# Two-layer hybrid backbone: the recurrent units hold their inverse and their transposed factors in tiles that they already have, and buffer and bank reserves are set anew

## The chip, the cores and the metric

One core of one Trainium2 chip runs the whole program. The metric is the device time of one execution in microseconds (us). The program is one launch with all weights in HBM; the profile shows one execution by the five engines of the core (TensorE, VectorE = DVE, ScalarE = ACT, GpSimd = POOL, SyncE = SP, which issues nearly all DMAs).

## What is computed

Two layers work on two streams of 256 tokens (context `s = 0`, latents `s = 1`), width 2048, all in float32. Each layer: a modulated RMS norm, one input projection (2048 x 5888), three head groups on its columns, a gate on each, one output projection (2048 x 2048), post norm and residual. Layer 1 gives only the latents, so of the context it needs only keys, values and the final recurrent state.

```python
def hybrid_layer(x, xc, c, c_ctx, cos, sin, lp, need_ctx_out):
    ...
    p = split_columns(h @ lp['w_in'])
    pc = split_columns(hc @ lp['w_in'])
    ...
    Sf_c, of_c = rwkv_scan(S0, r_c, vv_c, kk_c, *dirs_c[0], reverse=False)
    Sb_c, ob_c = rwkv_scan(S0, r_c, vv_c, kk_c, *dirs_c[1], reverse=True)
    _, of_l = rwkv_scan(Sf_c, r_l, vv_l, kk_l, *dirs_l[0], reverse=False)
    _, ob_l = rwkv_scan(Sb_c, r_l, vv_l, kk_l, *dirs_l[1], reverse=True)
    ...
    y = jnp.concatenate([att_l, rw_l, pool_l], axis=-1) @ lp['w_out']
```

The group that the change touches is the recurrence (`rwkv_scan`, 8 heads of 64, both directions): per token `S = S*w - (S kk)(kk a)^T + v k^T`, output `S r`.

## The kernel before

**A planner orders everything.** Each kind of work is a Python generator (`Worker`) that yields operations and tile requests. `Scheduler.run` (L543) keeps a model of engine times, takes at each step the ready operation that starts first in 40 ns slots with a bonus by priority (`PRIO`, L209: weight split and post norm 6, scan 5, back, elim, fin and attention 4, front 3, projection 0), and emits it; so each engine's instruction order is fixed when the program is built. All instructions are issued in one helper, so the profile gives line L587 (L332 for memsets) to nearly all of them, and groups are told apart by tile names. `HELD` (L207) is the extra time the model gives to an operation whose partitions start elsewhere than those of the one before on the same engine.

**Buffers.** Tile classes share pools (L121 to L130). `h`, `y`, `sp`, `wf`, `rf`, `rb`, `at`, `aq`, `lo`, `ev` and others take 2 KB slots of one pool of 77 (`SB_BYTES` less the constants and the other pools, L121). The PSUM classes `acc`, `ada`, `pr`, `scan`, `att`, `st` share 8 banks. `PHASES` (L131) gives each class a reserve in each phase: up to it a request is granted if a slot is free; beyond it only if the reserves that others haven't used still fit (`Scheduler.alloc`, L421). The sums of the reserves exceed 77 in the phases `first` to `second`, so there a class hardly gets more than its reserve. A request that isn't granted stops its worker, and a tile is free again when its last user is emitted. Phases in order: `start`, `turned`, `first` (layer 0 projections), `rested`, `between` (projection of layer 0 done), `turn` (first output pass prepared), `second` (set by `post_work` when the latents of layer 1 are modulated), `third` (layer 1 needs its context input no more), `last`.

**Projections.** `main_work` takes weight tiles (split by ACT into a rounded high part and by DVE into the rest, `w_split`) and issues three matmuls per 128 x 128 block: `acc<-h,sp` is the input projection (512 columns in layer 0, 256 per stream in layer 1), `acc<-sp,h` the output projection (512 columns), 384 matmuls for each of three passes (l, s) = (0, 0), (0, 1), (1, 1). Three column groups of layer 1's context part are issued ahead of the second half of pass (0, 1). The last pass needs the recurrence's rows last in its first half (`MIX_ORDER`).

**A recurrent unit** is (layer, head pair g, stream s): 16 units, 8 per layer, in the order of `UNITS`. Tokens are cut in four chunks of 64. Units run through five workers, one unit at a time in each:

- `front` (L1291): decays, keys and rates; fills `BK` (2 `rf` tiles), `W` (4 `rf` tiles, 2 where the unit gives no output, `need` false: the context units of layer 1), last `RS` (1 `rf` tile), from `psv`, a `pr` bank that it holds until `RS` is written. It asks for no `rf` tile until `back` has taken up the unit before.
- `back` (L1407): the products of `BK` and `W`, two `pr` banks per direction, masked by DVE into `UB` (2 `rb` tiles, 1 without `need`) and `W`; copies the diagonal 32 x 32 blocks to `N0`; transposes `BK` on TensorE into `W2` (2 `rb` tiles), frees `BK`; takes `Z` (1 `rb` tile) and clears it on POOL (L1455).
- `elim` (L1458): inverts the unit triangular diagonal blocks on DVE, 31 steps of two dependent operations (`tp<-dt,tp`, `tp<-tp`) after two large transposes (`dt<-tp`).
- `fin` (L1487): eight ACT copies of the inverted diagonal blocks into `Z`, then the off-diagonal blocks by 64 matmuls of 32 x 32 (`psY` from `UB`, `psZ`) and four ACT copies into `Z`. Without `need` it frees `UB`.
- `scan` (L1530): per chunk `psX` from `W` and `RS`, `psS` from `Z`, `psN` from `W2`, `psO` from `W` and `UB`, copies and state updates in between; at its end frees `RS`, `W`, `UB`, `W2`, `Z`; then a group norm and `rg_work`, whose result is a row of the output projection's input.

So a unit with output holds 7 `rf` tiles from `front` on, 5 of them and 5 `rb` tiles from the end of `back` to the end of `scan`. Without output these numbers are 5, then 3 `rf` and 4 `rb` (3 after `fin`). The reserves of `rf`/`rb` are 12/5 in `first` and `second`, 14/5 in `between` and `last`, 9/5 in `turn`.

Of the kernel before, what the change touches and what calls it, by code (L numbers as in the profile page):

```python
# [25 lines left out]
T = SEQ + CTX  # L26
# [75 lines left out]
def layout(a):  # L102
# [38 lines left out]
}  # L141
# [64 lines left out]
BACK = 60.0  # L206
HELD = 120.0  # L207
HOLD = {None: 1000.0, "ada": 3000.0}
# [418 lines left out]
class Hybrid:  # L627
# [779 lines left out]
    def back(self, l, g, s, need, RS, W, BK, PC, bv):  # L1407
        V, S, G, T, D_ = self.V, self.S, self.G, self.T, self.D
        ident = self.k("ident")
        UB = []  # L1410
# [28 lines left out]
        for q in range(4):  # L1439
            b = q % 2  # L1440
            for d in range(2):
                yield S.copy(out=N0[Q[q], d], in_=UB[d][Q[q], :, 0, 32 * b:32 * b + 32])
        W2 = []
        for d in range(2):
            z = yield Alloc("rb", (128, 4, 2, 64))
            W2.append(z)
            psW = yield Alloc("pr", (128, 512))
            for c in range(4):
                yield T.transpose(out=psW[:, 128 * c:128 * c + 128], in_=BK[d][:, c].rearrange("p a b -> p (a b)"), identity=ident)
            yield S.copy(out=W2[d].rearrange("p c h k -> p (c h k)"), in_=psW)  # L1450
            self.free(psW)
        self.free(*BK)

        Z = yield Alloc("rb", (128, 2, 4, 64))
        yield G.memset(out=Z, value=0.0)  # L1455
        self.push(self.bq, (N0, (l, g, s, need, RS, W, UB, W2, Z, PC, bv)))

# [28 lines left out]

    def fin(self, T1, T2, l, g, s, need, RS, W, UB, W2, Z, PC, bv):  # L1487
        V, S, G, T = self.V, self.S, self.G, self.T
        for q in range(4):
            b = q % 2  # L1490
            yield S.copy(out=Z[Q[q], 0, :, 32 * b:32 * b + 32], in_=T1[Q[q], 0].rearrange("p c u -> p u c"))
            yield S.copy(out=Z[Q[q], 1, :, 32 * b:32 * b + 32], in_=T2[Q[q], 1])
        psY = yield Alloc("pr", (128, 512))
        for u in range(4):
            for p in range(2):
                q0, q1 = Q[2 * p], Q[2 * p + 1]
                o = slice(32 * u, 32 * u + 32)
                yield T.matmul(out=psY[q1, o], lhsT=UB[0][q0, u, 0, 32:64], rhs=T2[q0, 0, u, :], start=True, stop=True)
                yield T.matmul(out=psY[q0, o], lhsT=UB[1][q1, u, 0, 0:32], rhs=T1[q1, 1, :, u], start=True, stop=True)
        YS = yield Alloc("tp", (128, 4, 32))  # L1500
        yield S.copy(out=YS.rearrange("p u t -> p (u t)"), in_=psY[:, 0:128])
        self.free(psY)
        psZ = yield Alloc("pr", (128, 512))
        for u in range(4):
            for p in range(2):
                q0, q1 = Q[2 * p], Q[2 * p + 1]
                o = slice(32 * u, 32 * u + 32)
                yield T.matmul(out=psZ[q0, o], lhsT=YS[q1, u, :], rhs=T1[q1, 0, :, u], start=True, stop=True)
                yield T.matmul(out=psZ[q1, o], lhsT=YS[q0, u, :], rhs=T2[q0, 1, u, :], start=True, stop=True)
        psz3 = psZ[:, 0:128].rearrange("p (u t) -> p u t", u=4)  # L1510
        for p in range(2):
            yield S.copy(out=Z[Q[2 * p], 0, :, 32:64], in_=psz3[Q[2 * p]])
            yield S.copy(out=Z[Q[2 * p + 1], 1, :, 0:32], in_=psz3[Q[2 * p + 1]])
        self.free(psZ, YS, T1, T2)
        if not need:
            self.free(*UB)
            UB = []
        self.push(self.pq, (l, g, s, need, RS, W, UB, W2, Z, PC, bv))

# [9 lines left out]

    def scan(self, Sc, l, g, s, need, RS, W, UB, W2, Z, PC, bv):  # L1530
        V, S, G, T, D_ = self.V, self.S, self.G, self.T, self.D
# [11 lines left out]
        for i in range(4):  # L1543
# [15 lines left out]
            for d in range(2):  # L1559
                for p in range(2):  # L1560
                    yield T.matmul(out=psS[H[p], 64 * d:64 * d + 64], lhsT=Z[H[p], d, c[d], :], rhs=X[H[p], 64 * d:64 * d + 64], start=True, stop=True)
            self.free(X)
# [35 lines left out]
            if need:  # L1598
# [5 lines left out]
                self.free(psO)  # L1604
        self.free(RS, *W[0], *W[1], *UB, *W2, Z, PC)
        if need:
# [340 lines left out]
```

## Time and profile before

| what | value |
|---|---|
| median of 3 executions | 1768.84 us (1763.94 to 1772.35) |
| profiled execution, its own time | 1770.03 us |
| its span, first to last instruction | 1768.1 us |
| mean granted TensorE clock | 0.981 |
| TensorE matmul busy | 1675.5 us (95%) |
| VectorE busy | 1350.8 us (76%) |
| ScalarE busy | 926.8 us (52%) |
| GpSimd busy | 16.0 us (1%) |
| DMA | 350.03 MB, mean 198 GB/s |

The profile's rows give a group's or an instruction's engine, line, operation, output tile `<-` input tiles, shape and count, with its time; "idle before" is the idle time of that engine ahead of it and what ended it. A busy TensorE is not one at its peak, since matmuls are pipelined and their ends modelled. Stages of the span: start and first modulation to 142 us; layer 0's input projection to 911; output passes (0, 0) and (0, 1) with the first groups of layer 1 to 1146; layer 1's input projection to 1633; output pass (1, 1) to 1756; post norm and stores to the end.

### The profile page before, as it was taken

To read this page: it belongs to the slowest core of one execution; us is meant where nothing else is said; L and a number is where in the kernel's file an instruction comes from. 1 tells how busy PE (TensorE), PEld (TensorE's weight loads), DVE (VectorE), ACT (ScalarE), POOL (GpSimd) and SP (SyncE) were. 2 spreads that over 40 slices of the span, in tenths; PEclk is the share of its full clock that TensorE was granted. 3 is DMA by queue.
4 is the path that set the end of the run, shared out by engine and by line. 5 is a ranking of instruction groups with operands and counts; after the bars stand their busy time and mean duration, and the time that the engine had idled before them with its cause. 6 is when DMAs were issued, how large, how long until landed. Compare 5 with 4: busy or idle time off the path is not lost.

```text
span 1768.1 us, 38232 instructions
## 1 busy us (share of the span) xinstructions
PE 1675.5 (95%) x13658; PEld 1330.3 (75%) x13658; DVE 1350.8 (76%) x4249; ACT 926.8 (52%) x2278; POOL 16.0 (1%) x93
## 2 busy tenths in 40 slices
PE   4999999999999999999999999999999999999977
PEld 3677677666766676667777888899999888888765
DVE  3335888867897869697767685899689999999863
ACT  5324455434554445345446574575455676666541
POOL 0000000000000000000000000000000000000000
PEclk9999999999999999999999999999999999999988
DMA  9993674657364945574669965665434536555642
GB/s 343 362 365 105 206 227 155 225 185 247 120 221 148 277 149 171 170 238 148 207 223 351 328 191 169 199 202 177 147 102 157 155 98 204 153 165 185 215 132 95
DMA packets 218094, 350.03 MB, mean 198 GB/s; under 512 B 22896, under 2 KB 62128, under 8 KB 217904
## 3 DMA queue, kind: packets, MB, share of 16 engines
q1 hardware_dynamic: 217904, 347.60, 60.2%
q8 instruction: 107, 1.75, 0.4%
q14 instruction: 83, 0.68, 0.1%
HBM read 316.54 MB, written 30.97 MB: 197 GB/s over the span
## 4 chain that ended last, share of the span: by engine, by line
PE 72%; DVE 12%; DMA 10%; ACT 2%; issue 2%; SPq 1%; DVEq 0%; POOL 0%; ACTq 0%
PE acc L587 50%; PE scan L587 6%; PE pr L587 5%; PE att L587 5%; PE ada L587 4%; DVE tp L587 3%; DMA wa<-in_ada_w_dram 2%; DVE sp L587 2%; DMA w<-in_ada_w_dram 2%; DVE q L587 1%; DVE rf L587 1%; DMA wf<-in_w_out_dram 1%; DMA wf<-in_w_in_dram 1%; PE st L587 1%; DMA sp<-w 1%
## 5 line engine op out<-in xcount | busy, mean ns | idle before, releaser
L587 PE MATMUL acc<-h,sp 128*128 128x256 f32 (+1 forms) x5088 | 971.1, 339 | 14.1 <-DMA sp<-w 5.6
L587 PEld LDWEIGHTS acc<-h,sp 128*128 128x128 f32 x5088 | 755.4, 190 | 133.9 <-issue 24.3
L587 DVE TENSOR_TENSOR sp<-wf,sp 128x512 fp32r<-128x512 f32 (+1 forms) x568 | 362.4, 664 | 96.4 <-ACT sp L587 90.2
L587 ACT CAST sp<-wf 128x512 fp32r<-128x512 f32 (+1 forms) x624 | 352.3, 603 | 20.8 <-PE acc L587 7.6
L587 PE MATMUL acc<-sp,h 128*128 128x512 f32 x1152 | 284.6, 403 | 2.9 <-DVE sp L587 2.9
L587 PEld LDWEIGHTS acc<-sp,h 128*128 128x128 f32 x1152 | 216.9, 191 | 54.1 <-DVE sp L587 3.8
L587 DVE TENSOR_TENSOR tp<-tp 128x48 f32<-128x48 f32 (+23 forms) x552 | 133.3, 247 | 5.6
L587 DVE TENSOR_TENSOR tp<-dt,tp 128x48 f32<-128x48 f32 (+23 forms) x496 | 112.0, 226 | 5.6
L587 PE MATMUL ada<-wa,cs 128*2 128x256 f32 x1024 | 85.8, 380 | 6.3 <-DMA wa<-in_ada_w_dram 6.2
L587 ACT CAST pw<-pw 128x512 fp32r<-128x512 f32 x56 | 34.8, 621 | 71.8 <-DMA pw<-in_w_in_dram 59.2
L587 ACT COPY sm<-scan 128x128 f32<-128x128 f32 x64 | 17.0, 265 | 104.4 <-PE scan L587 104.0
L587 DVE TENSOR_TENSOR rf<-tp 64x256 f32<-64x256 f32 x176 | 70.2, 421 | 0.4
L587 DVE STREAM_TRANSPOSE dt<-tp 128x1024 f32<-128x1024 f32 x32 | 65.7, 2077 | 0.0
L587 ACT ACTIVATE aq<-att,q 128x512 f32<-128x512 f32 (+1 forms) x48 | 33.9, 707 | 59.8 <-DVE q L587 49.7
L587 ACT COPY rf<-scan 64x128 f32<-64x128 f32 x128 | 33.2, 259 | 55.6 <-PE scan L587 50.8
L587 DVE SCALAR_TENSOR_TENSOR q<-q 128x4 f32<-128x4 f32 (+3 forms) x378 | 58.3, 159 | 4.2
L587 PEld LDWEIGHTS scan<-rf 128*64 128x64 f32 x896 | 37.3, 137 | 26.2 <-issue 9.2
L587 PE MATMUL ada<-w,cs 128*2 128x128 f32 x1024 | 37.0, 296 | 20.5 <-DMA w<-in_ada_w_dram 19.6
L587 DVE COPY adasb<-ada 2x128 f32<-2x128 f32 (+1 forms) x32 | 11.4, 357 | 57.4 <-ACT adasb L587 50.9
L587 DVE TENSOR_TENSOR pw<-pw 128x512 f32<-128x512 f32 x56 | 38.5, 687 | 21.6 <-ACT pw L587 21.3
L587 PE MATMUL scan<-rf 128*64 128x64 f32 x896 | 49.3, 230 | 4.4 <-DVE rf L587 4.1
L587 ACT COPY tp<-rb 32x128 f32<-32x128 f32 x128 | 37.5, 295 | 28.4 <-DVE rb L587 26.9
(154 smaller groups left out, 1965.7 us busy)
## 6 DMA issues: line engine op xcount, KB each, us to landing
wf<-in_w_in_dram SPq DMA_DIRECT2D x384, 256.0 KB, 3.8
wa<-in_ada_w_dram SPq DMA_DIRECT2D x256, 256.0 KB, 4.2
wf<-in_w_out_dram SPq DMA_DIRECT2D x192, 256.0 KB, 4.5
w<-in_ada_w_dram SPq DMA_DIRECT2D x128, 256.0 KB, 5.3
pw<-in_w_in_dram SPq DMA_DIRECT2D x56, 256.0 KB, 4.8
w<-pw SPq DMA_DIRECT2D x56, 256.0 KB, 2.5
sp<-w SPq DMA_DIRECT2D x56, 256.0 KB, 3.2
wf<-in_w_in_dram SPq DMA_DIRECT2D x48, 128.0 KB, 4.4
```

The costliest lines, as they stand in the source:

```text
L587: op.call(**op.args)
```

## The change

Three things are changed in the code, and the planner then draws up a new order for the whole program.

1. `Z` is gone. `UB`'s part `j = 0` (the masked product, whose other triangle is zero by the mask) takes the inverse: `fin` writes the diagonal blocks over it, computes `psY` from its off-diagonal blocks, and writes the new off-diagonal blocks over those. `scan` reads `psS` from `UB[d][.., c, 0, :]`. The POOL memset goes with `Z`. Units without `need` keep `UB` to the end of `scan`.
2. `W2` is gone. The transposes of `BK` are copied back into `BK`, so `BK` (2 `rf`) is held to the end of `scan`.
3. The reserves: `rf`/`rb` become 14/4 in `first`, `between`, `second` and `last`; in `turn` `rf`/`rb` go from 9/5 to 10/4, `y` from 14 to 12, `pr` from 2 to 3 and `scan` from 1 to 0. `HELD` goes from 120 to 118.5.

A unit with output so holds 7 `rf` and, from `back` on, 2 `rb` to the end of `scan`; one without output 5 and 1.

```diff
-    "first": {"pw": 2, "wf": 4, "wa": 4, "h": 32, "y": 1, "w2": 0, "xt": 0, "sp": (5, 12), "acc": 3, "st": (0, 2), "pr": 2, "scan": 2, "att": 1, "tp": 15, "ts": 2, "ta": 6, "tl": 2, "tu": 3, "rf": 12, "rb": 5, "lo": 4, "at": 8, "aq": 6},
+    "first": {"pw": 2, "wf": 4, "wa": 4, "h": 32, "y": 1, "w2": 0, "xt": 0, "sp": (5, 12), "acc": 3, "st": (0, 2), "pr": 2, "scan": 2, "att": 1, "tp": 15, "ts": 2, "ta": 6, "tl": 2, "tu": 3, "rf": 14, "rb": 4, "lo": 4, "at": 8, "aq": 6},
...
-    "turn": {"y": 14, "h": 34, "acc": 4, "st": 1, "ada": 0, "pr": 2, "scan": 1, "att": 0, "rf": 9, "rb": 5, "lo": 4, "at": 0, "aq": 0},
-    "second": {"sp": (4, 11), "tp": 16, "ta": 7, "tl": 0, "y": 1, "h": 32, "acc": 2, "ada": 0, "st": 0, "pr": 2, "scan": 2, "att": 1, "rf": 12, "rb": 5, "lo": 4, "at": 8, "aq": 6},
...
+    "turn": {"y": 12, "h": 34, "acc": 4, "st": 1, "ada": 0, "pr": 3, "scan": 0, "att": 0, "rf": 10, "rb": 4, "lo": 4, "at": 0, "aq": 0},
+    "second": {"sp": (4, 11), "tp": 16, "ta": 7, "tl": 0, "y": 1, "h": 32, "acc": 2, "ada": 0, "st": 0, "pr": 2, "scan": 2, "att": 1, "rf": 14, "rb": 4, "lo": 4, "at": 8, "aq": 6},
...
-HELD = 120.0
+HELD = 118.5
...
-        W2 = []
         for d in range(2):
-            z = yield Alloc("rb", (128, 4, 2, 64))
-            W2.append(z)
             psW = yield Alloc("pr", (128, 512))
             for c in range(4):
                 yield T.transpose(out=psW[:, 128 * c:128 * c + 128], in_=BK[d][:, c].rearrange("p a b -> p (a b)"), identity=ident)
-            yield S.copy(out=W2[d].rearrange("p c h k -> p (c h k)"), in_=psW)
+            yield S.copy(out=BK[d].rearrange("p c h k -> p (c h k)"), in_=psW)
             self.free(psW)
-        self.free(*BK)
-
-        Z = yield Alloc("rb", (128, 2, 4, 64))
-        yield G.memset(out=Z, value=0.0)
-        self.push(self.bq, (N0, (l, g, s, need, RS, W, UB, W2, Z, PC, bv)))
+        self.push(self.bq, (N0, (l, g, s, need, RS, W, UB, BK, PC, bv)))
...
-            yield S.copy(out=Z[Q[q], 0, :, 32 * b:32 * b + 32], in_=T1[Q[q], 0].rearrange("p c u -> p u c"))
-            yield S.copy(out=Z[Q[q], 1, :, 32 * b:32 * b + 32], in_=T2[Q[q], 1])
+            yield S.copy(out=UB[0][Q[q], :, 0, 32 * b:32 * b + 32], in_=T1[Q[q], 0].rearrange("p c u -> p u c"))
+            yield S.copy(out=UB[1][Q[q], :, 0, 32 * b:32 * b + 32], in_=T2[Q[q], 1])
...
-            yield S.copy(out=Z[Q[2 * p], 0, :, 32:64], in_=psz3[Q[2 * p]])
-            yield S.copy(out=Z[Q[2 * p + 1], 1, :, 0:32], in_=psz3[Q[2 * p + 1]])
+            yield S.copy(out=UB[0][Q[2 * p], :, 0, 32:64], in_=psz3[Q[2 * p]])
+            yield S.copy(out=UB[1][Q[2 * p + 1], :, 0, 0:32], in_=psz3[Q[2 * p + 1]])
         self.free(psZ, YS, T1, T2)
-        if not need:
-            self.free(*UB)
-            UB = []
...
-                    yield T.matmul(out=psS[H[p], 64 * d:64 * d + 64], lhsT=Z[H[p], d, c[d], :], rhs=X[H[p], 64 * d:64 * d + 64], start=True, stop=True)
+                    yield T.matmul(out=psS[H[p], 64 * d:64 * d + 64], lhsT=UB[d][H[p], c[d], 0, :], rhs=X[H[p], 64 * d:64 * d + 64], start=True, stop=True)
...
-        self.free(RS, *W[0], *W[1], *UB, *W2, Z, PC)
+        self.free(RS, *W[0], *W[1], *UB, *W2, PC)
```

## Rows read from the trace of the kernel before

**Rows 1.** Windows: us, PE, PEld, DVE, ACT, POOL busy (instructions), clock, DMA share, GB/s

```profile
1181.00:1350.00 169.00, 167.24 (x1580) 160.14 (x1578) 142.33 (x432) 93.66 (x225) 2.66 (x12) 1.00 0.48 149
1350.00:1633.00 283.00, 266.49 (x2679) 241.38 (x2682) 265.90 (x994) 190.98 (x517) 4.29 (x22) 0.99 0.49 153
1633.00:1685.00 52.00, 51.92 (x467) 38.83 (x455) 41.59 (x134) 26.64 (x67) 0.00 (x0) 1.00 0.64 214
1685.00:1702.50 17.50, 8.66 (x129) 6.76 (x128) 6.84 (x29) 3.06 (x11) 0.00 (x0) 0.76 0.22 71
...
142.00:911.00 769.00, 756.44 (x5832) 537.12 (x5833) 600.57 (x1963) 370.14 (x937) 7.50 (x46) 0.99 0.59 190
```

**Rows 2.** Chain that ended last, in order of time: start us, us, what

```profile
927.78 18.12 PE acc L587 x77
...
1682.83 2.28 PE acc L587 x9
1702.64 51.98 PE acc L587 x213
```

**Rows 3.** Timeline of ACT and PE, layer 0: a scan's last copies, next unit's back

```profile
274.23 0.53 ACT L587 COPY rf<-scan 64x128 f32<-64x128 f32 x2
276.64 1.16 PE L587 MATMUL pr<-rf 64*128 64x128 f32 x16
...
817.95 0.54 ACT L587 COPY rf<-scan 64x128 f32<-64x128 f32 x2 [0.71 <-PE scan L587]
820.48 1.16 PE L587 MATMUL pr<-rf 64*128 64x128 f32 x16
```

**Rows 4.** Timeline, unit (1, 2, 1): last copy into `RS`, first product of back

```profile
1504.44 0.26 ACT L587 COPY rf<-pr 64x128 f32<-64x128 f32 x1
...
1551.96 0.48 PE L587 MATMUL pr<-rf 64*128 64x128 f32 x2
```

**Rows 5.** Timeline of PE and POOL, layer 1's first two units

```profile
1122.00 1.11 PE L587 MATMUL pr<-rf 64*128 64x64 f32 x16
1125.23 0.38 PE L587 MATMUL pr<-c,tp 128*128 128x128 f32 x2
...
1181.36 0.46 POOL L332 MEMSET rf<- 64x128 f32 x2 [77.18 <-PE st L587]
...
1186.61 1.11 PE L587 MATMUL pr<-rf 64*128 64x64 f32 x16
```

**Rows 6.** Timeline of DVE: layer 1's first elimination, and the last one's end

```profile
1190.39 4.04 DVE L587 STREAM_TRANSPOSE dt<-tp 128x1024 f32<-128x1024 f32 x2
...
1240.42 0.17 DVE L587 TENSOR_TENSOR tp<-dt,tp 128x8 f32<-128x8 f32 x1
...
1657.60 0.16 DVE L587 TENSOR_TENSOR tp<-dt,tp 128x8 f32<-128x8 f32 x1
```

**Rows 7.** Windows with `scan` tiles alone: PE, PEld, DVE, ACT busy

```profile
1685.00:1702.50 17.50, 8.61 (x128) 6.76 (x128) 1.45 (x5) 2.35 (x9) 0.76 0.22 71
```

**Rows 8.** Windows after the gap, columns as in rows 1

```profile
1700.00:1705.00 5.00, 3.48 (x22) 2.91 (x23) 3.26 (x11) 1.29 (x3) 0.00 (x0) 0.50 0.01 3
```

**Rows 9.** Groups of DVE, 1190 to 1241 us: busy us, mean ns, idle before

```profile
L587 DVE TENSOR_TENSOR tp<-tp 128x48 f32<-128x48 f32 (+24 forms) x33 | 7.7, 237 | 0.4
L587 DVE TENSOR_TENSOR tp<-dt,tp 128x48 f32<-128x48 f32 (+23 forms) x31 | 7.0, 224 | 0.4
...
L587 DVE STREAM_TRANSPOSE dt<-tp 128x1024 f32<-128x1024 f32 x2 | 4.0, 2064 | 0.0
```

**Rows 10.** Windows at the turn to layer 1, columns as in rows 1

```profile
1135.00:1146.00 11.00, 11.00 (x50) 8.91 (x49) 5.42 (x10) 3.57 (x8) 0.00 (x0) 1.00 0.80 252
...
1170.00:1181.00 11.00, 9.32 (x62) 8.77 (x63) 9.80 (x30) 8.15 (x18) 0.00 (x0) 0.84 0.46 148
```

**Rows 11.** Timeline of ACT and PE, the last unit's `fin`

```profile
1660.44 1.88 ACT L587 COPY rb<-tp 32x128 f32<-32x128 f32 x6
1661.21 0.66 PE L587 MATMUL pr<-tp,rb 32*32 32x32 f32 x32
```

More of the change, by code (lines that the diff above doesn't have):

```diff
@@ L1485, in elim, with fin @@
         self.push(self.zq, (T1, T2) + unit)
-    def fin(self, T1, T2, l, g, s, need, RS, W, UB, W2, Z, PC, bv):
+    def fin(self, T1, T2, l, g, s, need, RS, W, UB, W2, PC, bv):
         V, S, G, T = self.V, self.S, self.G, self.T
@@ L1511, in fin @@
         for p in range(2):
-            yield S.copy(out=Z[Q[2 * p], 0, :, 32:64], in_=psz3[Q[2 * p]])
-            yield S.copy(out=Z[Q[2 * p + 1], 1, :, 0:32], in_=psz3[Q[2 * p + 1]])
+            yield S.copy(out=UB[0][Q[2 * p], :, 0, 32:64], in_=psz3[Q[2 * p]])
+            yield S.copy(out=UB[1][Q[2 * p + 1], :, 0, 0:32], in_=psz3[Q[2 * p + 1]])
         self.free(psZ, YS, T1, T2)
-        if not need:
-            self.free(*UB)
-            UB = []
-        self.push(self.pq, (l, g, s, need, RS, W, UB, W2, Z, PC, bv))
+        self.push(self.pq, (l, g, s, need, RS, W, UB, W2, PC, bv))
     def scan_work(self):
@@ L1528, in scan_work, with scan @@
                 self.phase("rested", "first")
-    def scan(self, Sc, l, g, s, need, RS, W, UB, W2, Z, PC, bv):
+    def scan(self, Sc, l, g, s, need, RS, W, UB, W2, PC, bv):
         V, S, G, T, D_ = self.V, self.S, self.G, self.T, self.D
```

4 rows, old and new, of the table PHASES are left out of this document.

## The prediction

> **What bounds the kernel now.** I read the windows by stage first. Through layer 0's projection, and through layer 1's up to 1350 us, TensorE is 98 to 99% busy; from 1350 to 1633 it is idle for 283 - 266.5 = 16.5 us while VectorE is busy for 265.9 of 283; from 1685 to 1702.5 it is busy for half the time, at a lower clock [rows 1]. The chain that ended last says why the last one matters: output matmuls stop at 1682.83 + 2.28 = 1685.1, and the closing run of 213 starts at 1702.64 [rows 2]. All that TensorE does in between is on `scan` tiles [rows 7]: the output pass waits for the last recurrent unit. So the program is TensorE's almost everywhere, and once, for 17.5 us, the recurrence's.
>
> Why is the recurrence late? Units follow each other too strictly. In layer 0 a unit's `back` starts 2 to 3 us from the last state copies of the unit before; the first and the last of seven such hand-overs are shown [rows 3], and the five between are alike to 3 us. The buffers explain it: one unit past `back` holds 5 `rb`, the whole reserve. In layer 1 unit (1, 2, 1) has its `RS` at 1504.7 and starts `back` at 1551.96, 47 us later [rows 4]. At layer 1's start there is a second hold: unit (1, 0, 0) has its first direction's products at 1122, its second's at 1186.61. In between, unit (1, 1, 0) has transposed `v` into `psv` at 1125.23 and gets `RS` only at 1181.36 [rows 5]. By the code that is `turn`'s 9 `rf`: 5 of one unit and 4 of the next; the tenth waits for `second`, and its owner sits on one of two `pr` banks.
>
> **The change, part by part.** Sums are made against the profiled execution: span 1768.1, own time 1770.0, 1.2 over the median of 1768.84; I apply the difference to the median.
>
> *Where the recurrence ends.* With 7 + 2 tiles per unit and 14 + 4 in reserve, two units can stand between `front` and the end of `scan`, where before it was one and the next one's `front`. Then `elim`, one unit at a time, paces it. Layer 1's eight eliminations run from 1190.39 to 1657.60, 467 us. One took 50 us (the first) [rows 6]. The eight have a middle of 42, an estimate from their starts and ends in the timeline, so back to back they need 8 x 42 = 336 us. From 1190 that ends at 1526, and 40 us for the last `fin` and `scan` give 1566, ahead of the projection's end at 1633. The tenth `rf` tile and the third `pr` bank in `turn` would start it up to 1186.6 - 1125 = 61 us earlier; I don't need that for the end, so its value there is nought. If the two-unit part failed, it alone would move 1702 ahead.
>
> *The gap.* Its 17.5 us go: -17.5. The unit's work in it isn't saved: 8.6 us of TensorE on `scan` tiles [rows 7] move into the projection, which is full: +8.6, an upper value, as these busy times overlap less when dense. The part of the chain between 1633 and 1685 moves too, at its own price: 0.
>
> *The clock.* After the gap the granted clock is 0.50, the lower of the two levels, 1.2 GHz [rows 8], since TensorE had little to do. The closing 213 matmuls take 51.98 us; at the pace of the dense run of 77 in 18.12 they take 50.1 [rows 2]. -1.9.
>
> *VectorE in layer 1.* The stretch to 1350 has 169 - 142.3 = 26.7 us of VectorE free, the next one 17.1 [rows 1]. Work that now sits in the second goes into the first, but eliminations from behind 1633 come in. TensorE's idle 16.5 us there may so go wholly or not at all: 0 to -16.5. I take -6, nearer to nothing because VectorE stays about as full.
>
> *The turn.* The first elimination moves from 1190 to about 1135, where `post_work` makes the latents' input. One elimination is 7.7 + 7.0 + 4.0 = 18.7 us of VectorE [rows 9]. The windows there have 5.6 and 1.2 us free, and in the second TensorE already idles for 1.7 of 11 us [rows 10], waiting for that input. What doesn't fit, 18.7 - 6.8 = 12 us, delays it at worst: 0 to +12. Post norm has priority 6 over 4 and most of an elimination's wall time is waiting, so I take +2. Queued behind on VectorE there are weight splits, for which the projection waits next.
>
> *`fin`.* The `psY` matmuls read a tile that the eight copies write, and the planner compares bounding boxes, so they wait for all copies. Before, they started at 1661.21 with copies running to 1662.32 [rows 11]: +1.1 us per unit of latency, behind which only that unit's `scan` waits. Covered by the 67 us from 1566 to 1633: 0; without that cover, +1.1 once, at the last unit.
>
> *Cheap edits.* 16 memsets leave POOL, busy for 2.66 us of 169 [rows 1]: 0. `W2` and `Z` copies go to other addresses with the same shapes: 0. Layer 0's recurrence ends earlier, but its projection has TensorE at 756.4 of 769 [rows 1]: 0, at best -12.6. No DMA is added or moved past a queue, save that rows of the output input are stored earlier. `HELD` reorders ties; nothing in the trace prices it, and I bound it by half the spread of the three executions, 4 us either way, taking 0.
>
> Sum: -17.5 + 8.6 - 1.9 - 6 + 2 = -14.8; 1768.8 - 14.8 = **1754 us**. What ends last then is the projection, 384 output matmuls and the post norm.
>
> A rule that speaks against it: the Trainium skill, Perfetto Trace Analysis, section Identifying the Most-Contended Engine, has one look for the most occupied engine and optimise that. TensorE is it, and no matmul goes, so by that rule the time stays at 1769. The trace disagrees for the 17.5 us in which that engine waits, and for no other stretch of that size.
>
> **The rivals.**
> *No gain that can be told (0.26).* The recurrence ends early, but VectorE doesn't absorb it: no relief (0), the turn collides at two thirds of its bound (+8). -17.5 + 8.6 - 1.9 + 8 = -2.8: 1766. For it: VectorE is 94% busy from 1350 and has about 1 us free in 11 at the turn. Against: 26.7 us are free right behind. Here also belongs that the change doesn't do what it says, two units still going one by one: 1769.
> *More gain (0.12).* All 16.5 us of idle time go, no collision: -17.5 + 8.6 - 1.9 - 16.5 = -27.3: 1741.5. For it: TensorE's waits there are for split weights, and two units in hand give the planner more to fill them with. Against: VectorE's load.
> *Slower (0.10).* Context units of layer 1 now keep 5 `rf` to the end, so three of them want 15 of `second`'s 14. The third, (1, 2, 0), gets all but `RS` and holds one of two `pr` banks until (1, 0, 0) leaves its scan; a `back` that still needs two banks stands as from 1125 to 1181 [rows 5], 56 us. The place is 1190 to 1320 us. It decides from the point where the last scan ends later than now (1695): a stop of 56 us against some 36 us won by pairing widens the gap by 20: 1789. For it: the same hold is in the trace once. Against: by then (1, 1, 0) should have passed `back`, and the recurrence has over 100 us in hand.
>
> **How the numbers follow.** The forecast has 0.52; alone it spans 1745 to 1762. The range reaches down past the larger gain with the 4 us for order, 1741.5 - 4 = 1737, and up over the no-gain case with the turn's full 12 us, 1768.8 - 17.5 + 8.6 - 1.9 + 12 = 1770; only the slower case and the very edges lie outside. About 0.5%, 8.8 us, is what a measurement of this kernel can tell from no change; below 1760 counts as faster. From the forecast a sliver over 1760 goes to no change, from the no-gain case a sliver to slower: faster 0.61, same 0.28, slower 0.11.
>
> **What would show it.** Right: in layer 0 `back` starts soon after its own `RS`, not at the other unit's scan end; `RS` of (1, 1, 0) near 1135; the last scan ends before 1633; from 1633 on output matmuls without a hole, clock 1.00. Wrong: a hole before the closing run; TensorE idle for over 5 us between 1146 and 1215 (the turn); `psv` held for tens of us behind 1190 (the slower case); a projection of layer 1 that ends later than 1642 (no gain).

## The result, and the profile after

The kernel after takes 1739.83 us (median of 4, 1737.11 to 1743.34) where before takes 1769.71 in the same comparison (4, 1763.94 to 1772.35): ratio 0.9837, 95% interval 0.9804 to 0.9869. It is faster by 30 us, twice the 15 us of the forecast, and inside the range near its lower end.

The stages, by the starts of the first and last projection matmuls (`acc<-h,sp`, `acc<-sp,h`) in the two timelines:

| us from the span's start | before | after | stage's change |
|---|---|---|---|
| layer 1's first projection matmul | 1055.4 | 1046.4 | -9.0 (layer 0, three quarters of its output passes) |
| last matmul of output pass (0, 1) | 1145.8 | 1142.2 | +5.4 (turn) |
| last matmul of layer 1's input projection | 1633.4 | 1628.2 | -1.6 |
| last matmul of output pass (1, 1) | 1754.9 | 1722.9 | -26.8 |
| span | 1768.1 | 1735.9 | -0.2 (post norm) |

TensorE's busy time goes from 1675.5 to 1666.7 us, so 8.8 of the 32.2 us of the span are busy time and 23.4 are time in which it stood still. The windows of after, with the columns of [rows 1]:

```profile
142.00:911.00 769.00, 757.36 (x5861) 543.66 (x5860) 605.62 (x1982) 373.24 (x943) 4.15 (x38) 1.00 0.59 191
...
1146.00:1181.00 35.00, 30.16 (x231) 29.20 (x230) 32.47 (x110) 23.49 (x51) 0.11 (x1) 0.90 0.70 242
1181.00:1350.00 169.00, 168.47 (x1681) 157.58 (x1680) 161.29 (x537) 98.19 (x247) 0.87 (x7) 1.00 0.43 132
1350.00:1628.00 278.00, 273.51 (x2821) 250.59 (x2820) 252.60 (x938) 192.14 (x510) 1.61 (x16) 0.99 0.53 167
1628.00:1685.00 57.00, 56.88 (x325) 44.35 (x324) 36.29 (x80) 28.13 (x65) 0.00 (x0) 1.00 0.76 247
1685.00:1702.50 17.50, 17.50 (x77) 14.15 (x76) 13.42 (x23) 10.34 (x20) 0.00 (x0) 1.00 0.59 186
```

Two of these stretches in before:

```profile
1146.00:1181.00 35.00, 32.99 (x261) 32.10 (x260) 32.14 (x89) 26.49 (x61) 0.00 (x0) 0.95 0.76 258
1350.00:1628.00 278.00, 262.85 (x2614) 238.52 (x2613) 261.30 (x979) 187.04 (x506) 4.29 (x22) 0.99 0.48 151
```

The stretch 1685 to 1702.5, half idle at a clock of 0.76 before [rows 1, 8], is full at 1.00. VectorE does 19 us more in 1181 to 1350 (161.3 against 142.3) and 9 us less behind it, and TensorE's idle time from 1181 to 1628 falls from 1.8 + 15.2 = 17.0 to 0.5 + 4.5 = 5.0 us. The turn's +5.4 us is moved work and no wait: TensorE is busy for 93.4 us of that stage, before for 88.0, with 64 matmuls of `back` more, and idles for 2.4 us in both. What the turn costs in waiting stands behind it: from 1146 to 1181 TensorE idles for 4.8 us, where it idled for 2.0.

The chain of after shows no hole before its closing run:

```profile
1646.47 8.55 PE acc L587 x36
1655.64 66.75 PE acc L587 x287
1728.86 3.97 DVE y L587 x6
```

The page's group of weight splits shows where VectorE had waited for ScalarE's half of the split (the last column). Before:

```profile
L587 DVE TENSOR_TENSOR sp<-wf,sp 128x512 fp32r<-128x512 f32 (+1 forms) x568 | 362.4, 664 | 96.4 <-ACT sp L587 90.2
```

After:

```profile
L587 DVE TENSOR_TENSOR sp<-wf,sp 128x512 fp32r<-128x512 f32 (+1 forms) x568 | 359.3, 661 | 31.7 <-ACT sp L587 22.8
```

**The units.** In layer 0 they overlap now. The tile views of `rf` on ACT to 1000 us have all state copies of layer 0's scans in one row, with first and last start. Before:

```profile
L587 ACT COPY rf<-scan x64: 247/260/262, 254.4 to 906.5; 64x128 f32<-64x128 f32 x64
```

After:

```profile
L587 ACT COPY rf<-scan x64: 246/261/262, 273.9 to 722.8; 64x128 f32<-64x128 f32 x64
```

The recurrence of layer 0 ends 184 us earlier. In the timelines of after, copies of unit (0, 1, 1) into `RS` and its first products of `back` stand 1 us apart, 43 us ahead of the last state copies of the unit before it; in [rows 3] `back` had to wait for another unit's scan end:

```profile
376.72 0.53 ACT L587 COPY rf<-pr 64x128 f32<-64x128 f32 x2 [1.23 <-PE pr L587]
...
377.71 1.16 PE L587 MATMUL pr<-rf 64*128 64x128 f32 x16
```

At the turn, unit (1, 1, 0) writes `RS` at 1117.93 (before, it got the tile at 1181.36 [rows 5] and wrote it at 1185.24) and starts `back` at 1122.92; the first elimination starts at 1125.68 (1190.39 in [rows 6]) and the last ends at 1589.58 (1657.60). The timelines of after:

```profile
1117.93 0.25 ACT L587 COPY rf<-pr 64x128 f32<-64x128 f32 x1
...
1122.92 1.19 PE L587 MATMUL pr<-rf 64*128 64x64 f32 x16
...
1125.68 2.21 DVE L587 STREAM_TRANSPOSE dt<-tp 128x1024 f32<-128x1024 f32 x1
...
1196.58 4.15 DVE L587 STREAM_TRANSPOSE dt<-tp 128x1024 f32<-128x1024 f32 x2
...
1589.58 0.17 DVE L587 TENSOR_TENSOR tp<-tp 128x8 f32<-128x8 f32 x1
```

So eight eliminations still take 464 us (467 before); they begin 65 us earlier. The time between one's end and the next one's start falls from 131 to 94 us in sum, as pairing should have it, but the eliminations get longer by as much, from 336 to 371 us in sum. (An elimination is counted from its first `dt<-tp` to its last `tp<-tp` in the timelines.) The first takes 71 us for 50: the second starts at 1196.58, as it ends.

### The profile page after: what moved, and what is told of

Its sections match the earlier page's. It is cut to its first block, busy times and chain, and to the rows that moved or that the text cites. A ratio compares the mean times of both kernels' runs of the same rounds, so it can differ in the third digit from the quotient of the medians.

```text
span 1735.9 us, 38175 instructions
## 1 busy us (share of the span) xinstructions
PE 1666.7 (96%) x13658; PEld 1331.2 (77%) x13658; DVE 1345.4 (78%) x4250; ACT 929.8 (54%) x2279; POOL 8.8 (1%) x77
## 4 chain that ended last, share of the span: by engine, by line
PE 78%; DMA 9%; DVE 8%; ACT 3%; issue 1%; SPq 0%; DVEq 0%; ACTq 0%
PE acc L587 56%; PE pr L587 6%; PE scan L587 5%; PE att L587 5%; PE ada L587 5%; DMA wa<-in_ada_w_dram 3%; DMA w<-in_ada_w_dram 2%; DVE tp L587 2%; DVE sp L587 2%; DMA wf<-in_w_in_dram 1%; DVE rf L587 1%; DMA pw<-in_w_in_dram 1%; PE st L587 1%; ACT sp L587 1%; DVE q L587 1%
## 5 line engine op out<-in xcount | busy, mean ns | idle before, releaser
L587 PE MATMUL acc<-sp,h 128*128 128x512 f32 x1152 | 278.9, 398 | 0.1
L587 DVE TENSOR_TENSOR tp<-tp 128x72 f32<-128x72 f32 (+21 forms) x552 | 134.0, 245 | 7.1 <-ACT tp L587 0.4
L587 PEld LDWEIGHTS scan<-rf 128*64 128x64 f32 x1344 | 56.9, 137 | 35.7 <-issue 10.2
L587 PE MATMUL scan<-rf 128*64 128x64 f32 x1344 | 77.5, 232 | 2.5 <-DVE rf L587 2.4
L587 ACT COPY adasb<-ada 2x128 f32<-2x128 f32 (+1 forms) x32 | 9.9, 310 | 84.4 <-PE ada L587 81.7
```

The costliest lines, as they stand in the source:

```text
L587: op.call(**op.args)
```

## Two ends that set the time

The output pass (1, 1) has two conditions, and all runs of this study can be read by them. **P** is the start of the last input projection matmul, **R** that of the last state copy of a scan, **O** that of the last output matmul. The tile views of `acc` and `rf` give them as "last start". Before:

```profile
L587 ACT COPY rf<-scan x64: 244/260/264, 1253.8 to 1695.2; 64x128 f32<-64x128 f32 x64
L587 PE MATMUL acc<-h,sp x2592: 274/281/562, 1146.0 to 1633.4; 128*128 128x256 f32 x200
L587 PE MATMUL acc<-sp,h x556: 387/394/793, 1099.7 to 1754.9; 128*128 128x512 f32 x186
```

After:

```profile
L587 ACT COPY rf<-scan x64: 243/261/263, 1216.1 to 1644.4; 64x128 f32<-64x128 f32 x64
L587 PE MATMUL acc<-h,sp x2592: 274/281/580, 1142.5 to 1628.2; 128*128 128x256 f32 x200
L587 PE MATMUL acc<-sp,h x525: 387/394/505, 1099.8 to 1722.9; 128*128 128x512 f32 x175
```

Behind P some 380 output matmuls are left; by the dense run of [rows 2] (77 in 18.12 us) they take 89 us, and with what else lies there it is 93. Behind R there are 213 of them, 52 us, and the unit's way to its row: 59. **O is the later of P + 93 and R + 59**, and the span ends 13 us behind O. The 93 and 59 are read off the runs themselves, so most rows agree by construction (the worst by 6 us). Four kernels (`first` of before, `rb` 6, `HELD` 119.5 twice) were run after the rule had been stated, and keep it to 3 us.

| kernel | median us, ratio to before | P | R | later of P + 93, R + 59 | O |
|---|---|---|---|---|---|
| before | 1769.71 | 1633.4 | 1695.2 | 1754.2 (R) | 1754.9 |
| after | 1739.83, 0.984 | 1628.2 | 1644.4 | 1721.2 (P) | 1722.9 |
| code alone | 1797.36, 1.015 | 1671.6 | 1724.5 | 1783.5 (R) | 1783.0 |
| after, `first` of before | 1810.82, 1.021 | 1702.9 | 1719.8 | 1795.9 (P) | 1798.4 |
| after, `turn` of before | 1771.01, 1.000 | 1662.5 | 1670.9 | 1755.5 (P) | 1754.0 |
| before, `turn` of after | 1768.19, 1.000 | 1650.7 | 1687.6 | 1746.6 (R) | 1748.7 |
| after, `HELD` 120 | 1755.34, 0.991 | 1645.4 | 1659.6 | 1738.4 (P) | 1738.5 |
| after, `HELD` 119.5 | 1741.99, 0.983 | 1633.7 | 1656.5 | 1726.7 (P) | 1728.7 |
| before, `HELD` 119.5 | 1792.05, 1.011 | 1654.4 | 1719.6 | 1778.6 (R) | 1778.3 |
| before, `HELD` 118.5 | 1820.52, 1.028 | 1717.6 | 1701.0 | 1810.6 (P) | 1805.2 |
| after, old `turn`, `at` 14 | 1757.83, 0.993 | 1622.0 | 1683.7 | 1742.7 (R) | 1742.6 |
| before, `at` 14 | 1834.66, 1.037 | 1601.7 | 1758.5 | 1817.5 (R) | 1817.9 |
| after, `at` 14 | 1748.19, 0.988 | 1633.8 | 1661.5 | 1726.8 (P) | 1732.9 |
| after, `rb` 6 | 1764.39, 0.995 | 1655.2 | 1656.9 | 1748.2 (P) | 1745.2 |

Before is bound by R, by 28 us: 17.5 of them are the hole, the rest TensorE's work for the late units in that pass and the lower clock behind the hole. After is bound by P, with 18 us to spare on R.

## The experiments

All twelve were timed in three rounds against before, whose median was 1771.29 to 1771.94 in these. The diffs are against after where nothing else is said.

**1. The code alone.** The edits of the functions, with every reserve and `HELD` of before.

```diff
...
-    "last": {"h": 16, "y": 14, "sp": 4, "acc": 4, "rf": 14, "rb": 4, "lo": 4, "at": 4, "aq": 6},
+    "last": {"h": 16, "y": 14, "sp": 4, "acc": 4, "rf": 14, "rb": 5, "lo": 4, "at": 4, "aq": 6},
...
-HELD = 118.5
+HELD = 120.0
```

`first`, `between`, `turn` and `second` are put back in the same way.

> The changed code with every reserve and HELD of the kernel before: rf 12 can hold one whole unit and five tiles of the next until a scan ends. P: units go one by one again in layer 0 and most of layer 1, the hole before the closing output run is back, 1758 to 1785 us. O: no relation to the reserves, 1745 to 1760 us.

Measured: 1797.36 us, ratio 1.0145 (1.0123 to 1.0168). The code alone is slower than before, and slower than either theory had it. A hole before the closing run is there, as P had it, of 7 us (from 1724.8). Layer 0's last scan ends at 978.7, and pass (0, 1) at 1190.1, 44 us later than before, which is more than the 28 us that the whole kernel loses.

**2. Only `first` put back.**

```diff
-    "first": {"pw": 2, "wf": 4, "wa": 4, "h": 32, "y": 1, "w2": 0, "xt": 0, "sp": (5, 12), "acc": 3, "st": (0, 2), "pr": 2, "scan": 2, "att": 1, "tp": 15, "ts": 2, "ta": 6, "tl": 2, "tu": 3, "rf": 14, "rb": 4, "lo": 4, "at": 8, "aq": 6},
+    "first": {"pw": 2, "wf": 4, "wa": 4, "h": 32, "y": 1, "w2": 0, "xt": 0, "sp": (5, 12), "acc": 3, "st": (0, 2), "pr": 2, "scan": 2, "att": 1, "tp": 15, "ts": 2, "ta": 6, "tl": 2, "tu": 3, "rf": 12, "rb": 5, "lo": 4, "at": 8, "aq": 6},
```

> The kernel after with the `first` reserves of before (`rf`/`rb` 12/5 for 14/4), nothing else. Theory A (a unit with output now keeps 7 `rf` to the end of its scan, so 12 hold one unit and not two): layer 0's units go one by one, the last scan of layer 0 ends at 970 to 985 (723 in after), layer 1's projection starts 35 to 45 us later, 1775 to 1805 us, ratio 1.003 to 1.02; then the larger reserve in `first` pays for the longer hold and is no gain of its own. Theory B (layer 0 is not what makes the kernel with the code alone slow; `second` and `turn` are): layer 0's last scan before 800, 1738 to 1755 us, ratio 0.982 to 0.992.

Measured: 1810.82 us, ratio 1.021 (1.0175 to 1.0245). The tile view of `rf` for its layer 0:

```profile
L587 ACT COPY rf<-scan x64: 247/261/264, 241.9 to 987.0; 64x128 f32<-64x128 f32 x64
```

Its windows, cut at the end of layer 0's projection, 894 in this kernel:

```profile
142.00:894.00 752.00, 734.84 (x5449) 523.03 (x5449) 573.34 (x1808) 353.14 (x881) 4.63 (x38) 1.00 0.61 194
894.00:987.00 93.00, 66.97 (x550) 52.34 (x549) 74.24 (x204) 44.20 (x107) 0.00 (x0) 0.79 0.52 169
```

The last copy is at 987.0, where after has 722.8. From 894 to 987 the output pass waits for units, TensorE stands for 26 us and its clock falls to 0.79. Pass (0, 1) ends at 1201.7, 59.5 us later than in after. Theory A's mechanism holds, and its numbers were too small by 2 us for the scan, 14 to 24 for the start of layer 1 and 6 for the time: since a unit with output keeps 7 `rf` to its end, 12 let only one go. The larger reserve first pays for the longer hold; what it gives over before's layer 0 is the 9 us of the stage table, since before's recurrence ended at 906.5, 6 us ahead of its projection.

**3 and 4. `turn`, both ways.** After with the `turn` line of before, and before with that of after:

```diff
-    "turn": {"y": 12, "h": 34, "acc": 4, "st": 1, "ada": 0, "pr": 3, "scan": 0, "att": 0, "rf": 10, "rb": 4, "lo": 4, "at": 0, "aq": 0},
+    "turn": {"y": 14, "h": 34, "acc": 4, "st": 1, "ada": 0, "pr": 2, "scan": 1, "att": 0, "rf": 9, "rb": 5, "lo": 4, "at": 0, "aq": 0},
```

> The changed kernel with only the reserves of the phase turn as before (y 14, pr 2, scan 1, rf 9, rb 5). Theory P (pairing: two units between front and the end of scan are what moves the recurrence ahead): the first elimination of layer 1 starts again near 1190 us, but the last scan still ends by about 1650 and the closing output matmuls run without a hole; 1740 to 1748 us. Theory T (the earlier start at the turn moved it; the eight eliminations of layer 1 took 463 us after the change and 467 before): the last scan ends near 1695 to 1705 again, a hole of over 10 us in the output pass comes back, 1755 to 1768 us.

> The kernel before with only the new reserves of turn (y 12, pr 3, scan 0, rf 10, rb 4). P: units still go one by one through back, rb 5 holds one of them; the chain starts up to 60 us earlier, ends 1650 to 1680, 1750 to 1765 us. T: the last scan ends near 1640 and nearly all of the gain is there, 1738 to 1748 us.

Measured: 1771.01 (1.0001, 0.9986 to 1.0016) and 1768.19 (0.9996, 0.9971 to 1.0021). On the new code `turn` is worth the whole gain; on the old code nothing: R comes 8 us earlier there and P 17 us later. The effects don't add, and both times fall outside the ranges of both theories. With the old `turn` on the new code the last scan comes 26 us later (R 1670.9), yet the closing pass has no hole: P comes 34 us later too. The window in which the projection stands:

```profile
1459.00:1516.00 57.00, 37.06 (x360) 28.96 (x361) 41.54 (x187) 25.83 (x78) 0.30 (x2) 0.55 0.08 25
```

The timeline of PE around it, from the last projection matmul to the next:

```profile
1458.51 0.36 PE L587 MATMUL acc<-h,sp 128*128 128x256 f32 x1
1466.21 0.45 PE L587 MATMUL scan<-rf 128*64 128x64 f32 x2 [7.34 <-DVE rf L587]
...
1473.73 0.39 PE L587 MATMUL pr<-tp,rb 32*32 32x32 f32 x10 [4.99 <-DVE tp L587]
...
1516.23 1.19 PE L587 MATMUL acc<-h,sp 128*128 128x256 f32 x8
```

For 57 us there is no projection matmul, DMA moves 25 GB/s, and TensorE runs recurrence and attention at their own pace. By the code a query group's `acc` bank is freed when ACT has copied it into `at` tiles. Here these copies come late; the timeline of ACT has two pairs from 1415 to 1500:

```profile
1455.24 0.39 ACT L587 ACTIVATE at<-acc 128x256 f32<-128x256 f32 x1
1455.52 0.48 ACT L587 ACTIVATE at<-acc,vecs 128x256 f32<-128x256 f32 x1
1493.13 0.39 ACT L587 ACTIVATE at<-acc 128x256 f32<-128x256 f32 x1
1493.89 0.47 ACT L587 ACTIVATE at<-acc,vecs 128x256 f32<-128x256 f32 x1
```

From `third` on the context's input is gone, slots are free beyond the reserves, and units that come late take them as `rf`; attention has 8 `at` reserved, all taken by keys and values. That was the theory for the next three.

**5 to 7. Slots for attention.**

```diff
-    "third": {"h": 16, "at": 8, "aq": 6},
+    "third": {"h": 16, "at": 14, "aq": 6},
```

On after with the old `turn`:

> The kernel after with the `turn` reserves of before (as in the first experiment, ratio 1.000), and in `third` 14 `at` tiles reserved for attention in place of 8. Theory A: with the old turn the units run later and sit, past their 14 `rf`, on the free slots that attention's query tiles need behind 1420 us; the query copies wait, their `acc` banks stay taken and the projection stands for 57 us between two groups. With `at` at 14 that pause shrinks below 15 us, the projection of layer 1 ends before 1645 (1662.5 without), and the ratio to before comes to 0.975 to 0.988 (1725 to 1748 us). Theory B (the order that the planner happens on, or the recurrence's own lateness, decides; attention's tiles are only in its wake): the pause stays over 25 us or moves to another group, ratio 0.994 to 1.005. Theory C (the late recurrence is what costs): the pause goes but a hole of over 10 us opens in the closing pass, ratio 0.99 to 0.995.

Measured: 1757.83, ratio 0.9925 (0.9898 to 0.9951). The window of the same stretch:

```profile
1459.00:1516.00 57.00, 55.29 (x509) 52.17 (x510) 55.06 (x234) 43.04 (x112) 0.28 (x4) 1.00 0.63 198
```

The first two pairs of those copies in its timeline of ACT:

```profile
1430.80 0.38 ACT L587 ACTIVATE at<-acc 128x256 f32<-128x256 f32 x1
1431.07 0.47 ACT L587 ACTIVATE at<-acc,vecs 128x256 f32<-128x256 f32 x1
1447.41 0.38 ACT L587 ACTIVATE at<-acc 128x256 f32<-128x256 f32 x1 [0.22 <-PE scan L587]
1452.59 0.47 ACT L587 ACTIVATE at<-acc,vecs 128x256 f32<-128x256 f32 x1
```

The copies come 24 and 46 us earlier, the longest pause between projection groups falls from 57 to 5 us, and P from 1662.5 to 1622.0, as theory A said. But its price for the whole, 0.975 to 0.988, was wrong: what attention gets the units lose, R goes from 1670.9 to 1683.7, and a hole of 10.9 us opens in the closing pass. That is theory C's mechanism and its interval.

On after, and on before:

> The kernel after, `third` at 14 `at` tiles. Theory A: after has only some 6 us of pauses between projection groups, so there is little left to win: 1732 to 1742 us, ratio 0.979 to 0.985. Theory B: another order by chance, anywhere from 1735 to 1760 us, ratio 0.981 to 0.995.

> The kernel before, `third` at 14 `at` tiles, nothing else. Theory A: before has pauses of some 20 us between projection groups and a hole of 17.8 us in the closing pass that comes from the late recurrence; the pauses shrink to under 10 us and the hole stays or grows, since the units lose slots: 1752 to 1768 us, ratio 0.990 to 0.999. Theory B: 1765 to 1780 us, ratio 0.997 to 1.006. If it comes below 1745 us, the tile change was not needed for the gain at all.

Measured: 1748.19 (0.9881, 0.9858 to 0.9904) and 1834.66 (1.0366, 1.0334 to 1.0397). On after nothing was to be won by it and 8 us are lost: outside theory A's interval, inside that of theory B (another order). On before P falls by 32 us to 1601.7, the earliest of all, and R rises by 63 to 1758.5; no theory had the size. Its windows, from P on:

```profile
1602.00:1646.00 44.00, 42.99 (x211) 32.90 (x210) 43.26 (x129) 22.62 (x51) 1.06 (x2) 1.00 0.54 172
1646.00:1766.00 120.00, 52.66 (x676) 42.19 (x674) 65.84 (x245) 27.55 (x94) 0.00 (x0) 0.55 0.09 28
1766.00:1818.00 52.00, 52.00 (x216) 41.87 (x216) 25.48 (x43) 21.05 (x44) 0.00 (x0) 0.96 0.36 116
```

It is the picture of [rows 2, 7] seven times as long: 120 us in which TensorE does the last three units alone, then the 52 us of the closing run. So this reserve trades one end against the other. The same reserve costs R 13 to 17 us with the new code and 63 with the old; by the code a unit with output holds 9 tiles (7 `rf`, 2 `rb`) from `back` on, where it held 10, and 11 for a moment in `back`.

**8. More `rb` in layer 1.** In after `back` of (1, 3, 0) and (1, 2, 1) still start at 1405.2 and 1493.0, with their own `RS` at 1379.2 and 1447.8; another unit's scan ends then, and by the code 4 `rb` are two units.

```diff
...
-    "last": {"h": 16, "y": 14, "sp": 4, "acc": 4, "rf": 14, "rb": 4, "lo": 4, "at": 4, "aq": 6},
+    "last": {"h": 16, "y": 14, "sp": 4, "acc": 4, "rf": 14, "rb": 6, "lo": 4, "at": 4, "aq": 6},
```

`second` is changed in the same way.

> The kernel after with 6 `rb` in `second` and `last` for 4, so that in layer 1 a `back` need not wait for the end of the scan before. Theory A (the end is the later of two: projection end + 93 and last scan + 59; in after the projection decides): the last scan ends earlier (before 1640, 1644 in after), the slots it takes are attention's and the projection ends at 1630 to 1660, so no gain: 1738 to 1770 us, ratio 0.982 to 1.0. Theory B (what I predicted from: two units in flight pace the recurrence, and its pace is the time): 1720 to 1735 us, ratio 0.971 to 0.980.

Measured: 1764.39, ratio 0.9948 (0.9927 to 0.9969). Theory B falls: with more units in flight the kernel loses 1.1 points of the gain of 1.6%. Theory A has the time and P (1655.2), but not R: (1, 2, 1) starts `back` at 1486.1, 7 us earlier, yet the last scan ends at 1656.9 and not before 1640. The eliminations run from 1126.1 to 1597.7, no closer together, and the projection pays: it stands for 25 us from 1400.8 and for 12 us from 1461.3, where 8 us is its longest stop in after. The windows around them, in which TensorE idles for 5.6 and 4.3 us at a lower clock:

```profile
1400.00:1426.00 26.00, 20.40 (x157) 16.74 (x156) 19.04 (x84) 8.49 (x26) 0.11 (x1) 0.67 0.11 33
1461.00:1501.00 40.00, 35.68 (x401) 31.15 (x399) 33.41 (x117) 22.61 (x65) 0.21 (x2) 0.87 0.36 111
```

**9 to 12. `HELD`.** It adds to the planner's time of every copy or vector operation whose partitions change, so another value draws another order of the whole program.

```diff
-HELD = 118.5
+HELD = 120.0
```

The diff is that of after with 120; before with 118.5, and both with 119.5, are made alike.

> The changed kernel with HELD at 120.0. If that constant only breaks ties: within 5 us of the changed kernel (1735 to 1746). Rival O (order: a good part of the gain is the luck of one order of instructions): over 8 us slower than the changed kernel.

> The kernel before with `HELD` at 118.5 in place of 120 and nothing else. If `HELD` has an effect of its own on the order (the 15 us that it gives on the kernel after are its worth), the ratio is 0.988 to 0.995 (1750 to 1762 us). If it only breaks ties, and its 15 us on the kernel after are luck of one order, the ratio lies within 0.995 to 1.008 on either side of one.

> The kernel after with `HELD` at 119.5, a value that neither kernel has. If the tiles that a unit needs are what gives the gain, and `HELD` only draws another order: 1738 to 1756 us, ratio 0.982 to 0.992. If 118.5 is a lucky order that carries the gain: 1760 us or more, ratio above 0.994.

> The kernel before with `HELD` at 119.5. If the tiles are what counts, it stays behind the kernel after at the same `HELD` by 15 us or more: 1768 to 1805 us, ratio 0.999 to 1.02. If the order decides, it may come out anywhere, below 1755 us (ratio under 0.991) too.

| `HELD` | before | after | after less before |
|---|---|---|---|
| 118.5 | 1820.52 | 1739.83 | -81 |
| 119.5 | 1792.05 | 1741.99 | -50 |
| 120.0 | 1769.71 | 1755.34 | -14 |

The ratios to before are 0.9912 (0.9893 to 0.993), 1.0278 (1.0258 to 1.0298), 0.9828 (0.9803 to 0.9853) and 1.0106 (1.0076 to 1.0137). For 118.5 on before both readings had missed: it is no gain and no tie-break but a loss of 51 us. In its trace the projection stands twice in the way of experiment 3, without a projection matmul in most of either stretch:

```profile
1500.00:1538.00 38.00, 24.70 (x270) 20.03 (x269) 18.43 (x70) 14.19 (x46) 0.28 (x4) 0.60 0.13 43
1611.00:1678.00 67.00, 42.38 (x517) 32.30 (x516) 53.25 (x235) 29.36 (x92) 0.00 (x0) 0.54 0.07 23
```

In after at 120, too, there is such a stop, of 26 us, and P comes 17 us later than at 118.5:

```profile
1491.50:1517.60 26.10, 19.45 (x149) 15.64 (x147) 21.94 (x71) 13.42 (x41) 0.28 (x4) 0.68 0.12 36
```

So `HELD` has no sign of its own. Tiles and reserves win at each of the three values, by 14 to 81 us; the spread over the values is 51 us for before and 16 for after. Before stands at the best of the three values for its own code, and after at one of the two best, which can't be told apart (1737.11 to 1743.34 us and 1740.92 to 1743.56); so the 30 us of the result compare two good orders. None of the kernels tried is faster than after.

## Why the prediction was right, and where it failed

The time lies in the range, 14 us below the forecast. The hole went, as forecast, and most of the gain is there. But the recurrence came early for another reason than the one that the sum rests on, and the range has 4 us for the planner's order, which alone moves after by 16 us (experiments 9 and 11). That the time lies in the range is in part luck.

**The hole and what stands behind it: right, too small.** The forecast took 17.5 + 1.9 = 19.4 us off the closing pass, and it got 26.8 shorter. Missing is the recurrence's work between 1633 and 1685, whose way into the projection I set at nought: in after 325 matmuls run from 1628 to 1685, where before ran 467 in 52 us [rows 1]. For the projection I had +8.6 for the moved work and -6 for relief, +2.6; it measured -1.6. The relief term was mis-sized: of TensorE's idle time 12 us went, about three quarters of the bound of 16.5, while VectorE was no less busy there on the whole (161.3 + 252.6 = 413.9 against 142.3 + 261.3 = 403.6). I had held the relief small for VectorE's sake, and taken these waits to be for split weights; by TensorE's waits from 1181 to 1628 those were less than half, and fell from 7.4 to 1.7 us, while those for recurrence and attention fell from 8.9 to 3.1. The rival with all the relief, 1741.5, came nearest to the time, but it left the turn without cost and layer 0 as it was.

**"Then `elim`, one unit at a time, paces it", 336 us, last scan by 1566: wrong.** The eliminations take 464 us and the last scan ends at 1644. The working took each at 42 us with nothing between them; with two units in flight they take 46 us in the mean and 94 us lie between. In experiment 8, with more units in flight, it is 47 and 99; what each waits for was not followed. What came true is the sentence that the sum didn't use, by which the earlier start at the turn moves the end if pairing fails. There was no hole all the same, since a last scan up to P + 93 - 59 = P + 34 = 1662 stays hidden. My test "the last scan ends before 1633" was some 30 us too strict.

**The turn's worth "nought": wrong.** It rested on the 67 us of cover from 1566 to 1633. The cover in after is 18 us, and without the new `turn` the gain is gone (experiment 3), and not by the recurrence's end: P + 34 is 1696 there, so its R of 1670.9 would stay hidden, but the projection stands for 57 us. That units which come late may cost the projection has no term in the sum. The collision, +2 (0 to +12), may show in the 2.8 us more idle time of TensorE from 1146 to 1181, in which it waits for `y` of the post norm; that the elimination delays `y` is not shown, since VectorE is as busy there as before (32.5 and 32.1 us). From 1146 to 1215 the idle time is 5.1 us, at my sign of being wrong (over 5).

**Layer 0 "0, at best -12.6": in the bounds.** It gave 9.0. What I didn't see is the other side: with 12 `rf` the code costs 59.5 us there (experiment 2). Counting 7 + 7 against the old reserve would have shown it.

**`HELD`, 4 us either way: the step that failed by most in time.** At 120 after takes 1755.34 us, 1 us from the forecast, though not by its terms: the four stages change by -5.1, +5.5, +11.6 and -28.4 us there, against my 0, +2, +2.6 and -19.4. From there to 118.5 it is 15.5 us, and for before 51. I had bounded it by the spread of repeated executions of one order, which says nothing of another order.

**The slower rival's hold is there.** Unit (1, 2, 0) transposes `v` into its bank at 1207.29 and empties it into `RS` only from 1251.61 on, while (1, 0, 0) ends its scan; the bank is held for 44 us. Timelines of after:

```profile
1207.29 0.38 PE L587 MATMUL pr<-c,tp 128*128 128x128 f32 x2
...
1251.61 0.26 ACT L587 COPY rf<-pr 64x128 f32<-64x128 f32 x1
```

But (1, 1, 0) had passed `back`, as the rival's counter-argument had it, and TensorE is busy for 168.5 of the 169 us around it.

**"No matmul goes, so 1769".** The Trainium skill (Perfetto Trace Analysis, Identifying the Most-Contended Engine) has one optimise the engine with the highest occupancy first. That this leaves the time at 1769 where no matmul goes was my own reading, and it failed: 23.4 of the 32.2 us were time in which that engine waited, so the change worked on TensorE's waits.

**What stays open.** Which of the slots an order hands out at a given `HELD` decides was not followed. That attention's tiles cause the pause was forecast and borne out for after with the old `turn`, in one order; for the stops of before at 118.5, of after at 120 and of experiment 8 it is argued from a like picture. Experiments 1 to 8 have one order each, and three values of `HELD` spread after by 16 us and before by 51. Experiments 2 (71 us), 3 (31), 7 (65) and 8 (25) go beyond that; the nought of experiment 4 and the 13 and 8 us of 5 and 6 don't, and could be the order's. Before's code with 14 and 4 was not tried, since one of its units needs 5 `rb`; nor was it with 14 and 5, by which larger reserves alone would be a rival. `Z` and `W2` were not taken apart, nor the reserves of `second`, `between` and `last`.

## What to carry to other kernels

Ask of a late chain not only when it ends but how late it may end: count the work that can run without it, and do the same for the stage it hides behind; here two sums, P + 93 and R + 59, read fourteen kernels. A buffer that one worker gets is one that another lacks, so price a reserve at both ends, and with each reserve count how many whole units fit. Where a planner draws the order, compare two versions at several values of a neutral constant: a single pair showed 14 or 81 us for the same edit.

## What the hardware showed that was not expected

The clock falls in the middle of a busy program, too, and then stretches the very chain that TensorE waits for. In the pause of experiment 3 TensorE is busy for 37 of 57 us and the granted clock is 0.55 in the mean, close to the lower level of 1.2 GHz; in the hole of before with `at` 14 it is 0.55 for 120 us. In the pause 16 products of a scan take 1.53 to 1.54 us, against 14 of the same shape in 0.69 in after at 1254, at full clock (1.00 from 1181 to 1350). Two such groups in the pause, timeline of PE:

```profile
1485.96 1.54 PE L587 MATMUL scan<-rf 128*64 128x64 f32 x16 [0.86 <-DVE rf L587]
...
1491.26 1.53 PE L587 MATMUL scan<-rf 128*64 128x64 f32 x16 [0.79 <-DVE rf L587]
```

The one of after:

```profile
1254.39 0.69 PE L587 MATMUL scan<-rf 128*64 128x64 f32 x14
```

So a stop of the dense matmuls costs more than the waits that it consists of.
